# Input weights of a hybrid mixer: the low part made by a negated cast on ScalarE and an adding DMA instead of a subtract on VectorE

## The chip, the cores and the metric

The kernel runs on one core of one Trainium2 chip. The metric is the device time in microseconds of one execution of the whole program. Engines are named as in the profile: PE is the matrix engine (TensorE), DVE is VectorE, ACT is ScalarE, POOL is GpSimd, SP issues most of the DMAs.

## The reference, cut to what matters

One inference step of a decoder block runs on 512 prompt tokens and 8 sample tokens (520 columns, handled as two halves of 260): a half-step SwiGLU feed-forward network (FFN), a mixer, a second FFN, and a final norm. The change touches the first product of the mixer:

```python
def _hybrid_mixer(h, pool_prefix, conv_prefix, ssm_h0, start_pos, w_in, ...):
    proj = h @ w_in
    u_pool, z, xbc, dt_raw = jnp.split(proj, [POOL_DIM, POOL_DIM + SSD_DIM, ...], axis=-1)
    pool_out, new_pool = _pool_mix(u_pool, ...)
    xbc_act, new_conv = _causal_conv(xbc, ...)
    ...
    return cat @ w_out, ...
```

`w_in` has 1024 rows. Its columns, apart from the 16 of `dt`, are 24 blocks of 128: 4 for B and C (bc0 to bc3), 8 for x (x0 to x7), 4 for the pooling mixer (p0 to p3) and 8 for the gate z (z0 to z7). Everything is float32 and has to be accurate to nearly that.

## The kernel before, in words

PE multiplies numbers of the shorter type float32r at one fast pass. To keep accuracy, each operand is split in a high part (the value cast to float32r) and a low part (the rest), and a product is three products: high by high, high by low, low by high (`mm3`, lines 121 to 126). The activations of the mixer are split in `prep` (lines 140 to 146): ScalarE writes `xh` (line 143), VectorE writes `xl` (line 144).

One block of `w_in` is one unit: a weight tile of 128 partitions by 1024 columns, 512 KB. `inproj` (line 709) loads it with `load_unit` (line 116) and issues 48 matmuls of 260 columns: two halves, eight blocks of 128 rows, three products each. In them `whi` stands in lines 122 and 125 and `wlo` in line 126. `load_unit` takes a raw tile, starts the load from SP's queue (line 118), and hands the tile to `split`. `split` (line 101) casts it on ScalarE to `whi` (line 106), and makes the low part in one of two ways. Without `late`, VectorE subtracts the cast from the raw tile (line 113). With `late`, ScalarE writes the negative of the cast of the raw tile into `wlo` (line 109), and a DMA from POOL's queue reads the weights in DRAM a second time and adds them to that tile (line 110); the sum is the same rest. Both FFNs use the second way already for a part of their tiles, in pieces of 128 x 512 or 128 x 384. The mixer's input weights and output weights use the first.

The tags `whi` and `wlo` have three buffers each, so a unit takes the buffer of the third unit before it, once PE is through with that. Raw tiles come in pairs: two units share one allocation of two halves, and there are two such pairs, so a raw pair is loaded again once both its halves have been read.

The order of the mixer's stages is written by hand in three plans. The first, `CONV_PLAN`, starts

```python
    "b0 b1 d0 b2 b3 x0 x1 v0 d1 x2 x3 d2 X0 p0 y0 c0 A0 p1 x4 m0 x5 B0 c1 p2 m1 A1 x6 c2 p3 A2 B1 x7 "
```

where b, x and p are the units above with what follows them (convolution with a ring of columns that POOL prepares, lines 796 to 812; pooling sums on POOL, lines 828 to 846), A and B are the two halves of the state space scan for one chunk and head group (`ssd_a`, `ssd_b`), and c and m are the centring and mixing of the pooling branch. `GATE_PLAN` interleaves the z units with the rest of the scan, the sample tokens (s), the gates (G, H) and the output product (o, g); `LAST_PLAN` ends the mixer and starts the second FFN. A scheduler then places the instructions on each engine's queue, so the order on an engine differs from the written one; every engine works its own queue strictly in order. Before the first unit stand the `dt` products (lines 734 to 739), which need the last chunk of `xh` and `xl`, and the banks of PSUM that the first FFN's last evacuations (line 478) leave.

Banks of PSUM are emptied by VectorE: a unit by lines 719 to 721 (or 1051 for z), the scan's transposes by line 1008 and others, an output product by line 1061.

Of the kernel before, what the change touches and what calls it, by code (L numbers as in the profile page):

```python
# [17 lines left out]
D = 1024  # L18
# [43 lines left out]
def tile_trunk_step(ctx: ExitStack, tc: tile.TileContext, ins: dict, outs: dict):  # L62
# [7 lines left out]
    wp = ctx.enter_context(tc.tile_pool(name="wp", bufs=3, side="right"))  # L70
# [24 lines left out]
    def raw_tile(name):  # L95
        if not half:
            t = raw_pair(name)
            half.extend([t[:, 1], t[:, 0]])
        return half.pop()

    def split(src, n, name, hp, nb, tags, late=None):
        hi, lo = (hp.tile([P, 1024], F32R, tag=t, bufs=nb, name=f"{t}_{name}")[:, :n] for t in tags)
        h, l = hi, lo
        if len(src.shape) == 3:
            h, l = (t.rearrange("p (j c) -> p j c", j=src.shape[1]) for t in (hi, lo))
        nc.scalar.copy(h, src)  # L106
        q = 0 if late is None else n - late.shape[1]
        if late is not None:
            nc.scalar.activation(out=lo[:, q:], in_=src[:, q:], func=AF.Copy, scale=-1.0)
            nc.gpsimd.dma_start(out=lo[:, q:], in_=late, accum_op=ALU.add)  # L110
        if late is None or q:
            s = slice(0, q) if late is not None else slice(None)
            nc.vector.tensor_tensor(out=l[:, s], in0=src[:, s], in1=h[:, s].bitcast(F32), op=ALU.subtract)
        return hi, lo

    def load_unit(src, n, name):
        raw = raw_tile(name)[:, :n]
        nc.sync.dma_start(out=raw, in_=src)
        return split(raw, n, name, wp, 3, ("whi", "wlo"))

    def mm3(ps, whi, wlo, xhi, xlo, start, stop, pin=False, **kw):
        first = nc.tensor.matmul(ps, whi, xhi, start=start, stop=False, **kw)  # L122
# [81 lines left out]
    class Ffn:  # L204
# [257 lines left out]
        def down(self, c, lo, hi, after):  # L462
            n = hi - lo
            banks, units = {}, {}

            def part(d, ks):
                if d not in units:
                    units[d] = load_unit(ins[f"w{self.i}d"][d, :, lo * P : hi * P], n * P, f"{self.i}d{d}_{c}")
                    banks[d] = ps[0].tile([P, 2, 512], F32, tag="BE", bufs=2, name=f"dn{self.i}_{d}_{c}")
                wh, wl = units[d]  # L470
                for b in range(2):
                    for k in ks:
                        g = self.g[lo + k]
                        mm3(banks[d][:, b, :HB], ws(wh, k), ws(wl, k), g[:, 0, b], g[:, 1, b], k == 0, k == n - 1)

            def done(d):
                for b, hs in enumerate(HALVES):
                    nc.vector.tensor_tensor(out=h[:, d, hs], in0=banks[d][:, b, :HB], in1=h[:, d, hs], op=ALU.add)
                    after(d, b, hs)

            part(0, range(n - 1))
            part(1, range(n - 1))
            part(0, range(n - 1, n))
            done(0)
            part(1, range(n - 1, n))
            done(1)
            for d in range(2, KD):
                part(d, range(n))
                done(d)
# [139 lines left out]
    todo, late = [], []  # L629
# [48 lines left out]
def mixer(tc, ins, outs, e):  # L678
    nc = tc.nc
    cst, act, wp, tmp, dr, pool = (e[x] for x in ("cst", "act", "wp", "tmp", "dr", "pool"))  # L680
    ones = e["ones"]
    bank, load_unit, mm3, ws, v, rstd, rstds, vec, h, nx2, raw_tile, open_f2, fin, fill = (
        e[x] for x in ("bank", "load_unit", "mm3", "ws", "v", "rstd", "rstds", "vec", "h", "nx2", "raw_tile",
                       "open_f2", "fin", "fill"))
# [22 lines left out]
    ncp = mp.tile([P, 12, 3], F32, tag="ncp", name="ncp")  # L707

    def inproj(src, name):
        wh, wl = load_unit(src, D, f"in{name}")  # L710
        bs = [bank(f"in{name}{b}") for b in range(2)]
        for b, hs in enumerate(HALVES):
            for k in range(KD):
                mm3(bs[b][:, :HB], ws(wh, k), ws(wl, k), xh[:, k, hs], xl[:, k, hs], k == 0, k == KD - 1)
        return bs
# [111 lines left out]
    def pooling(g):  # L827
        w = WINDOWS[g]
        bs = inproj(ins["w_in"][12 + g], f"p{g}")
        U = cv[0].tile([P, LP], F32, tag="cu", bufs=6, name=f"PU{g}")  # L830
        us = U[:, SAMPLE_P:LP].rearrange("p (b j) -> p b j", j=16)
# [214 lines left out]
    def zproj(j):  # L1046
        if not zbox:
            zbox.append(cv[0].tile([P, NX, NT], F32, tag="zs", name="zs"))
        bs = inproj(ins["w_in"][16 + j], f"z{j}")
        for b, hs in enumerate(HALVES):  # L1050
            nc.vector.tensor_tensor(out=zbox[0][:, j, hs], in0=bs[b][:, :HB], in1=r[:, hs], op=ALU.mult)
# [55 lines left out]
    def outs_a():  # L1107
# [4 lines left out]

    stages = {
        "b": lambda j: conv(8 + j, inproj(ins["w_in"][j], f"bc{j}"), BC[:, j]),
        "x": lambda j: conv(j, inproj(ins["w_in"][4 + j], f"x{j}"), X[:, j]),
        "d": lambda j: box.update(dta=token_dt()) if j == 0 else (token_acs(box["dta"]), sample_decay()) if j == 1 else head_acs(),
# [118 lines left out]
```

## Time and profile before

| what | value |
|---|---|
| median of three runs | 984.54 us (983.57 to 985.28) |
| the profiled execution | 984.47 us |
| its span, first to last instruction | 982.6 us |
| granted clock of PE, mean | 0.997 |
| busy share PE, DVE, ACT, POOL | 97%, 89%, 69%, 22% |
| DMA | 145.46 MB moved, mean 148 GB/s |

A row of a timeline gives the start in us from the span's start, the length in us, the engine, the line, the operation, the tile written and the tiles read, the shape, the count, and in brackets how long the engine had been idle and what ended that. A row of stretches gives the stretch, its length, the busy time of PE, of the weight loads of PE, of DVE, ACT and POOL with counts, the granted clock, the busy share of the DMA engines and the GB/s. A row of groups gives the line, engine and operation, the count, and after the bar the busy time, the mean length of one in ns and the idle time before them. A DMA row gives the issues, the KB of each and the median us from issue to landing.

### The profile page before, as it was taken

Reading aid. Unit: us, or ns where it says so; the run is one execution under the profiler, and the core shown is the slowest. Engines: PE = TensorE matmul, PEld = TensorE weight load, DVE = VectorE, ACT = ScalarE, POOL = GpSimd, SP = SyncE. Lnnn points to the kernel's source line nnn. Section 1 sums busy time; section 2 is a strip of 40 time slices with the busy share of each in tenths; the row PEclk is TensorE's granted clock in tenths of the full one; section 3 lists DMA queues with packets and bytes.
Section 4 is the critical chain, followed back from the end, with each engine's and each line's share of the span. In section 5 each row is a group of like instructions: output and inputs, shape, how many; then the busy total and the mean of one; then the engine's idle time right before and its main releaser. Section 6 shows DMA issues by size and latency. Waiting matters only on the chain.

```text
span 982.6 us, 20242 instructions
## 1 busy us (share of the span) xinstructions
PE 951.5 (97%) x7636; PEld 927.4 (94%) x7636; DVE 877.8 (89%) x1624; ACT 678.2 (69%) x1263; POOL 217.9 (22%) x319
## 2 busy tenths in 40 slices
PE   7999999999999999999999999999999999999995
PEld 6899999999999999999899998989999999999995
DVE  7899899989989698788979987999999999999976
ACT  7677677677777475685754335678788888888864
POOL 0112211121121000157411000113333233233300
PEclk9999999999999999999999999999999999999998
DMA  5565766576566243262335232456687768767732
GB/s 182 161 172 114 191 161 143 133 186 175 124 149 165 65 148 119 87 210 86 115 120 165 96 115 90 106 152 164 164 213 185 183 156 223 190 155 189 190 91 88
DMA packets 63571, 145.46 MB, mean 148 GB/s; under 512 B 9257, under 2 KB 22505, under 8 KB 63473
## 3 DMA queue, kind: packets, MB, share of 16 engines
q1 hardware_dynamic: 41168, 103.78, 33.2%
q0 software_dynamic: 22304, 40.38, 22.5%
q8 instruction: 60, 0.98, 0.4%
q14 instruction: 39, 0.31, 0.1%
HBM read 136.80 MB, written 7.34 MB: 147 GB/s over the span
## 4 chain that ended last, share of the span: by engine, by line
PE 85%; DVE 8%; ACT 3%; issue 2%; DMA 1%; POOL 1%; SPq 0%; DVEq 0%; ACTq 0%
PE A L126 7%; PE A L122 7%; PE A L125 7%; PE BE L122 6%; PE BE L125 6%; PE BE L126 6%; PE P L311 3%; PE wo L122 2%; PE wo L125 2%; PE wo L126 2%; PE inz L122 2%; PE A2d L125 2%; PE A2d L126 2%; PE A1d L125 2%; PE A1d L126 2%
## 5 line engine op out<-in xcount | busy, mean ns | idle before, releaser
L380 ACT COPY ac<-A 128x260 f32<-128x260 f32 x123 | 45.1, 369 | 16.8 <-PE A L126 16.5
L311 PE MATMUL P<-xg_f,raw 128*128 128x260 f32 x192 | 45.9, 398 | 5.5 <-DMA raw<-in_w1gu 5.5
L346 DVE TENSOR_TENSOR s<-raw 128x1024 f32<-128x1024 f32 x41 | 49.8, 1216 | 1.4 <-DMA raw<-in_w2gu 1.4
L311 PEld LDWEIGHTS P<-xg_f,raw 128*128 128x128 f32 x192 | 37.5, 199 | 11.5 <-ACT xg_f L188 5.4
L943 POOL DMA_DIRECT2D out_nss<-hs x32 | 20.6, 643 | 79.2 <-DVE hs L961 74.0
L106 ACT CAST whi_wo<-raw_wo 128x1024 fp32r<-128x1024 f32 x12 | 12.5, 1046 | 36.5 <-issue 9.2
L125 PE MATMUL wo<-catg,whi_wo 128*128 128x260 f32 x128 | 36.4, 285 | 1.3 <-DVE catg L1092 1.3
L122 PE MATMUL wo<-catg,whi_wo 128*128 128x260 f32 x128 | 37.3, 292 | 0.3 <-DVE h L1061 0.3
L122 PE MATMUL inz<-xh_mx,whi_inz 128*128 128x260 f32 x128 | 36.8, 288 | 0.0
L122 PE MATMUL inx<-xh_mx,whi_inx 128*128 128x260 f32 x128 | 36.4, 285 | 0.0
L126 PE MATMUL wo<-catg,wlo_wo 128*128 128x260 f32 x128 | 36.3, 284 | 0.0
L126 PE MATMUL inz<-xh_mx,wlo_inz 128*128 128x260 f32 x128 | 36.2, 283 | 0.0
L126 PE MATMUL inx<-xh_mx,wlo_inx 128*128 128x260 f32 x128 | 36.2, 283 | 0.0
L125 PE MATMUL inz<-xl_mx,whi_inz 128*128 128x260 f32 x128 | 36.2, 283 | 0.0
L125 PE MATMUL inx<-xl_mx,whi_inx 128*128 128x260 f32 x128 | 36.1, 282 | 0.0
L392 DVE TENSOR_TENSOR tg<-BE,ac 128x520 f32<-128x520 f32 x41 | 28.3, 691 | 5.2 <-PE BE L126 5.2
L807 DVE SCALAR_TENSOR_TENSOR A<-U,h,A 128x544 f32<-128x544 f32 x36 | 28.0, 778 | 4.3 <-ACT A L805 3.3
L401 DVE TENSOR_TENSOR tg<-tg,r_f 128x520 f32<-128x520 f32 x41 | 28.4, 694 | 1.3 <-ACT tg L399 1.0
L398 DVE TENSOR_TENSOR tg<-tg,r_f 128x520 f32<-128x520 f32 x41 | 28.4, 692 | 0.1
L347 DVE TENSOR_TENSOR s<-s,raw 128x512 f32<-128x512 f32 x41 | 28.0, 682 | 0.0
L348 DVE TENSOR_TENSOR s<-s,raw 128x512 f32<-128x512 f32 x41 | 27.9, 681 | 0.0
L399 ACT ACTIVATE tg<-tg 128x520 f32<-128x520 f32 x41 | 26.1, 637 | 1.0 <-DVE tg L398 0.9
(1787 smaller groups left out, 4747.4 us busy)
## 6 DMA issues: line engine op xcount, KB each, us to landing
raw<-in_w2gu SPq DMA_DIRECT2D x44, 512.0 KB, 4.9
raw<-in_w1gu SPq DMA_DIRECT2D x42, 512.0 KB, 4.7
raw_1d<-in_w1d SPq DMA_DIRECT2D x24, 384.0 KB, 4.0
raw_2d<-in_w2d SPq DMA_DIRECT2D x24, 384.0 KB, 4.0
raw_wo<-in_w_out SPq DMA_DIRECT2D x12, 512.0 KB, 4.8
ab<-scr_acs SPq DMA_DIRECT2D x8, 512.0 KB, 4.4
h<-in_state_ssm SPq DMA_DIRECT2D x16, 256.0 KB, 3.8
raw_inz<-in_w_in SPq DMA_DIRECT2D x8, 512.0 KB, 4.1
```

The lines of the kernel that those rows point to most:

```text
L122: first = nc.tensor.matmul(ps, whi, xhi, start=start, stop=False, **kw)
L125: nc.tensor.matmul(ps, whi, xlo, start=False, stop=False, **kw)
L126: nc.tensor.matmul(ps, wlo, xhi, start=False, stop=stop, **kw)
L311: nc.tensor.matmul(self.banks[f, u][b][:, :HB], ws(self.raw[f][:, u], j + 4 * q), xg[:, slot[q]], start=j == q == 0, stop=j == 3 and q == ...
L346: nc.vector.tensor_tensor(out=s1, in0=diag, in1=up0, op=ALU.add)
L347: nc.vector.tensor_tensor(out=s2[:, 0], in0=s1[:, 1], in1=raw[:, 0, :nb], op=ALU.add)
L348: nc.vector.tensor_tensor(out=s2[:, 1], in0=s2[:, 0], in1=raw[:, 0, nb : 2 * nb], op=ALU.add)
L380: nc.scalar.copy(keep, out[:, :HB])
L392: nc.vector.tensor_tensor(out=tg, in0=self.BE[k][:, :, :HB], in1=a, op=ALU.add)
L398: nc.vector.tensor_tensor(out=tg, in0=tg, in1=r, op=ALU.mult)
L401: nc.vector.tensor_tensor(out=tg, in0=tg, in1=r, op=ALU.mult)
L807: nc.vector.scalar_tensor_tensor(out=A[:, :n], in0=U[:, j : j + n], scalar=w(j), in1=A[:, :n], op0=ALU.mult, op1=ALU.add)
```

## The change

`load_unit` takes a `late` argument and hands it to `split`, and `inproj` gives the weights in DRAM for it, for every unit but bc0. So 23 of the 24 input units get their low part from a ScalarE write of the negated cast (line 109) and an adding DMA of 512 KB from POOL's queue (line 110), and 23 subtracts of line 113 go from VectorE. The output weights keep the subtract. Line numbers stay the same.

```diff
-    def load_unit(src, n, name):
+    def load_unit(src, n, name, late=None):
         raw = raw_tile(name)[:, :n]
         nc.sync.dma_start(out=raw, in_=src)
-        return split(raw, n, name, wp, 3, ("whi", "wlo"))
+        return split(raw, n, name, wp, 3, ("whi", "wlo"), late)
...
     def inproj(src, name):
-        wh, wl = load_unit(src, D, f"in{name}")
+        wh, wl = load_unit(src, D, f"in{name}", None if name == "bc0" else src)
```

The scheduler's new order keeps PE's almost as it was. On ScalarE each negation stands right behind the cast of its unit, except that those of bc1 and bc2 stand one cast earlier, between the last norm chunks. On POOL the 23 issues are spread between the ring copies, the pooling sums and the scan's products. On VectorE the instructions around the 23 subtracts move up.

## The prediction

> **What bounds the kernel now.** I read the page's busy shares first, then its chain of work, then the busy time by stretches, then who waits for whom on PE.
>
> ```profile
> span 982.6 us, 20242 instructions
> PE 951.5 (97%) x7636; PEld 927.4 (94%) x7636; DVE 877.8 (89%) x1624; ACT 678.2 (69%) x1263; POOL 217.9 (22%) x319
> ...
> PE 85%; DVE 8%; ACT 3%; issue 2%; DMA 1%; POOL 1%; SPq 0%; DVEq 0%; ACTq 0%
> ```
>
> PE is busy 97% of the span and is 85% of the chain that ended last. The change gives PE no less work (its matmuls are the same and stand in nearly the same order), so it can only act through PE's waits. How many are there in the mixer (about 360 to 600 us)? The busy time by stretches, columns PE, PEld, DVE, ACT, POOL:
>
> ```profile
> 335.00:420.00 85.00, 82.53 (x679) 80.77 (x678) 68.00 (x143) 51.41 (x92) 7.68 (x35) 1.00 0.31 105
> 420.00:475.00 55.00, 53.79 (x454) 50.70 (x453) 48.67 (x101) 39.09 (x82) 36.66 (x58) 1.00 0.46 151
> 475.00:530.00 55.00, 54.58 (x458) 51.55 (x459) 49.50 (x140) 32.73 (x60) 12.02 (x12) 1.00 0.39 126
> 530.00:632.00 102.00, 98.86 (x748) 93.50 (x747) 89.58 (x215) 46.78 (x62) 6.76 (x7) 1.00 0.33 104
> ```
>
> PE idles 2.5, 1.2, 0.4 and 3.1 us: 7.2 us in 297. That is the ceiling of any gain. VectorE is 80 to 90% busy, ScalarE 46 to 71%: the work moves from the fuller engine to the emptier one, but neither sets the end; PE does. PE's waits one by one, in the order of time:
>
> ```profile
> 360.74 0.29 PE L737 MATMUL dt<-xh_mx,w 128*48 128x260 f32 x1 [1.35 <-DVE dt_v L757]
> ...
> 472.53 1.09 PE L1027 MATMUL yd<-ab,xdt 128*64 128x128 f32 x16 [0.35 <-DVE U L719]
> 474.20 0.30 PE L976 MATMUL pb<-ident,BC 128*128 128x128 f32 x1 [0.58 <-DVE U L721]
> 475.38 0.55 PE L984 MATMUL px<-ident,X 128*128 128x128 f32 x3 [0.66 <-DVE xdt L1008]
> 579.03 1.15 PE L168 MATMUL psr_y<-X,ones 128*128 128x260 f32 x4 [1.56 <-ACT X L1083]
> 595.07 0.39 PE L125 MATMUL wo<-catg,whi_wo 128*128 128x260 f32 x1 [0.62 <-DVE catg L1092]
> 598.55 0.39 PE L125 MATMUL wo<-catg,whi_wo 128*128 128x260 f32 x1 [0.63 <-DVE catg L1092]
> 599.58 0.39 PE L122 MATMUL wo<-catg,whi_wo 128*128 128x260 f32 x1 [0.28 <-DVE h L1061]
> ```
>
> No wait is for an input weight: those tiles are ready early. Seven of the eight are for VectorE, which the change relieves.
>
> **What the change removes and adds.** The subtracts it removes and the casts that stay, each as the busy time of one line in one stretch (stretch, its length, busy time and count, clock, DMA share, GB/s), and a small precedent:
>
> ```profile
> 360.00:515.00 155.00, 30.04 (x23) 1.00 0.37 123
> ...
> 360.00:515.00 155.00, 23.26 (x23) 1.00 0.37 123
> L109 ACT ACTIVATE wlo_3a<-raw 128x512 fp32r<-128x512 f32 x1 | 0.6, 625 | 0.0
> ```
>
> The first row is line 113 alone: 23 subtracts, 30.0 us of VectorE. The second is line 106: 23 casts, 1.01 us each. The new ScalarE write has half-size precedents at 625 ns (third row); between that and twice that, 1.25 us, I take the cast's 1.04 us: 23 x 1.04 = 24 us more on ScalarE. On POOL come 23 issues, bounded and priced by these rows:
>
> ```profile
> L110 POOL DMA_DIRECT2D wlo_1b<-in_w1gu x1: 846/846/846, 31.4 to 31.4; - x1
> ...
> DMA to landing us min/median/max: 3.4/4.9/9.2
> raw_inz<-in_w_in SPq DMA_DIRECT2D x8, 512.0 KB, 4.1
> raw_1d<-in_w1d SPq DMA_DIRECT2D x8, 256.0 KB, 3.2
> wlo_1a<-in_w1gu POOLq DMA_DIRECT2D x1, 256.0 KB, 3.9
> ```
>
> An issue holds POOL 0.85 us (20 us in all). No adding DMA of 512 KB is in the trace. An adding one of 256 KB took 3.9 us, and doubling a plain load cost 4.1 - 3.2 = 0.9 us, so I take 4.8, say 5 us, with 3.4 and 9.2 (the ends of the 126 existing ones) as bounds.
>
> The Trainium skill, "DMA: Bandwidth & Descriptors", section "Anatomy of one DMA — SWDGE (gpsimd) path", fits about 2.0 us plus bytes/436e3 for a DMA issued from GpSimd; by that estimate 512 KB would land in 3.2 us, below the fastest 256 KB one here (3.4), so the trace's rows decide. With 3.2 us the sum stays as it is and only the slower rival loses weight.
>
> **Does the longer path reach PE?** The low tiles have three buffers, so a unit's buffer is freed when the third unit before it is done. The tightest is x1, which takes over from bc2:
>
> ```profile
> 383.88 0.28 PE L126 MATMUL inbc<-xh_mx,wlo_inbc 128*128 128x260 f32 x1
> ...
> 395.75 0.28 PE L126 MATMUL inx<-xh_mx,wlo_inx 128*128 128x260 f32 x1
> ```
>
> bc2 ends at 383.88 + 0.28 = 384.16, and x1's first low product comes at 395.75: 11.6 us. The new path is cast 1.04, negation 1.04, DMA 5: 7.1 us. Cover is left of 4.5 us; with a landing of 9.2 it is 11.3, still inside. Units further on have transposes and scan products between them and more room. In POOL's new order each of these DMAs stands behind the ring copies of the unit before (0.2 us each) and ahead of the evacuation copies, and later behind the pooling sums. The longest such queue is before p2:
>
> ```profile
> 435.56 0.64 POOL L843 TENSOR_TENSOR PW<-PW,rcnt 128x3 f32<-128x3 f32 x1
> 440.76 0.29 PE L126 MATMUL inp<-xh_mx,wlo_inp 128*128 128x260 f32 x1
> ```
>
> p2's DMA now follows that line 843, which ended at 436.2. Two more issues (x4, x5) stand before it, but the products it waits for come from a less loaded VectorE (two subtracts fewer, 2.6 us), so I put its issue at about 435 and its landing at 440: in time by under 1 us. Bounds: 0, and 3 us of PE wait if the issue slips to 438.5. I take 0; behind the issue on POOL stand the sums of p1 and the copies of x4, which PE does not need soon.
>
> **Step 1, the seam from the first FFN: a loss.** Two negations (bc1, bc2) now stand on ScalarE ahead of the last two norm chunks:
>
> ```profile
> 357.38 0.51 ACT L143 ACTIVATE xh_mx<-h 128x260 fp32r<-128x260 f32 x1
> ...
> 359.31 1.04 ACT L106 CAST whi_inbc<-raw_inbc 128x1024 fp32r<-128x1024 f32 x1 [0.39 <-PE dn L125]
> ...
> 359.84 0.75 DVE L478 TENSOR_TENSOR h<-dn,h 128x260 f32<-128x260 f32 x2
> 360.30 0.51 ACT L143 ACTIVATE xh_mx<-h 128x260 fp32r<-128x260 f32 x1
> ...
> 362.00 0.48 DVE L144 SCALAR_TENSOR_TENSOR xl_mx<-h,xh_mx 128x260 fp32r<-128x260 f32 x1
> ```
>
> The chunk cast at 357.38 moves to 358.4, the one at 360.30 by both negations less the idle 0.39 before the second cast, to about 362. Its low part, no longer behind a subtract, goes from 362.00 to 362.45 and ends at 362.9. PE's dt products start when line 478 frees the banks; VectorE's new order puts that ahead of one low part, so about 0.4 us earlier (360.35). Fourteen products at 0.12 us (54.58 us over 458 in the stretches above) bring PE to 362.05, where it waits for the low part until 362.95: 0.9 lost, 0.4 won, **+0.5 us**. Bounds: -0.4 (no wait) and +1.7 (all of the delay).
>
> **Step 2, the waits at 472 to 475: a gain.** VectorE is behind by then:
>
> ```profile
> 461.24 1.99 DVE L113 TENSOR_TENSOR wlo_inz<-raw_inz,whi_inz 128x1024 fp32r<-128x1024 f32 x1
> ...
> 473.56 0.41 DVE L720 TENSOR_TENSOR U<-inx,r_mx 128x252 f32<-128x252 f32 x1
> ...
> 474.64 0.68 DVE L1008 TENSOR_TENSOR xdt<-px,tok 128x512 f32<-128x512 f32 x1
> ```
>
> VectorE empties x7's bank only at 473.6 to 474, and the next transposes wait. Without the subtracts of p3, x7, z0 and z1 (4 x 1.3 us, 30.04 over 23) it comes there earlier, and in its new order the evacuation is ahead of four of the scan's subtractions. The 0.35 + 0.58 + 0.66 go: **-1.6 us**. Bounds: 0 and -1.6.
>
> **Step 3, the last gate: part of the waits.** At 579.03 PE waits for squares that ScalarE makes after a weight cast, itself tied to PE's release of a buffer, and after the gate products:
>
> ```profile
> 577.40 1.04 ACT L106 CAST whi_wo<-raw_wo 128x1024 fp32r<-128x1024 f32 x1 [4.73 <-DVE X L1075]
> 578.35 2.60 ACT L1083 ACTIVATE X<-zs 128x520 f32<-128x520 f32 x4
> 589.68 1.21 DVE L113 TENSOR_TENSOR wlo_wo<-raw_wo,whi_wo 128x1024 fp32r<-128x1024 f32 x1
> 596.62 1.21 DVE L113 TENSOR_TENSOR wlo_wo<-raw_wo,whi_wo 128x1024 fp32r<-128x1024 f32 x1
> ```
>
> That cast and its order stay, so I leave the 1.56 us where it is. After it, the new VectorE order takes the subtract at 596.62 from ahead of the last gated low part (the 0.63 goes), and one evacuation from ahead of the first (part of the 0.62; I take 0.37): **-1.0 us**. Bounds: 0 and -3.1 (all four waits).
>
> Sum: 0.5 - 1.6 - 1.0 = -2.1 us. The profiled execution took 984.47 us (1.87 around its span), close to the median of 984.54. 984.47 - 2.1 = **982.4 us**.
>
> **Rivals.**
> - More: the gates end early enough that the 1.56 us goes too: 982.4 - 1.6 = 980.8. For it: the subtracts of z6 and z7 (2.7 us) leave VectorE's last crowded stretch. Against it: the cast at 577.40.
> - No gain: 24 us more in order on ScalarE make its products late where VectorE's were, and the waits only change their name: 984.47 + 0.5 = 985.0, up to 986. For it: ScalarE is 71% busy from 420 to 475 (row above). Against it: of PE's waits above, one names ScalarE, and that one late.
> - Slower: the adding DMAs land late, beside 1 MB raw loads that each second negation sets free. It decides from a path of 11.6 us, thus a landing plus POOL wait above 9.5 us after the negation. With 10.2 us each of the seven back-to-back units bc3 to p1 waits up to 0.7 us: 7 x 0.7 = 5, time 982.4 + 5 = 987.4. For it: the 9.2 in the row. Against it: the median of 4.9 and a DMA share of 0.3 to 0.46 here.
> - VectorE holds POOL: if the scan's tensor_scalar runs kept POOL from issuing for as long as they last (8 of them, 2.2 us), p2 would leave at 437 and PE wait about 1.3 us: 983.7.
>
> ```profile
> 427.45 2.19 DVE L1003 TENSOR_SCALAR ab<-ab,tok 128x128 f32<-128x128 f32 x8
> ```
>
> The Trainium skill, "SBUF — State Buffer", section "Who interferes with whom", says that tensor_scalar can take a mode that locks GpSimd out of the shared port, descriptor generation included. No issue stands beside such a run in this trace, so it shows neither.
>
> **How the numbers follow.** Forecast 0.47 (own range 981.0 to 983.8), more 0.13, no gain 0.15, VectorE holding POOL 0.08, slower 0.17. 0.2% of 984.54 is 1.97 us, about what a measurement of this kernel tells from no change: faster is below 982.57, slower above 986.51. Faster: 0.30 of the forecast's 0.47 and all of "more": 0.43. Same: 0.17, 0.08, and 0.11 of "no gain": 0.36. Slower: 0.04 and 0.17: 0.21. The range 980.5 to 987.0 leaves out about 0.05 below and 0.10 above.
>
> **What would show it.** Right: no PE wait on an input weight's DMA; the rows at 472 to 475 without their waits; a dt product waiting about 0.9 us; 23 POOL issues landing in 4.5 to 7 us. Wrong: PE's weight loads waiting for the low tiles, above all at p2 and x1; ScalarE named in new waits between 420 and 480; landings above 9 us.

## The result, and the profile after

| | median us (lowest to highest, runs) | profiled execution |
|---|---|---|
| before | 984.71 (983.57 to 985.68, 6) | 984.47 |
| after | 990.14 (989.37 to 993.55, 6) | 989.69 |

The changed kernel is 0.6% slower: the ratio is 1.0061, 95% interval 1.0045 to 1.0077. The prediction was 982.4 in a range of 980.5 to 987.0. From the page of after: span and instructions, busy time by engine, and the queue of the DMAs that POOL issues (packets, MB, share of the 16 DMA engines).

```profile
span 987.6 us, 20290 instructions
...
PE 953.9 (97%) x7636; PEld 928.8 (94%) x7636; DVE 854.6 (87%) x1601; ACT 699.9 (71%) x1286; POOL 227.1 (23%) x342
...
q0 software_dynamic: 25616, 52.44, 29.2%
```

The same queue before:

```profile
q0 software_dynamic: 22304, 40.38, 22.5%
```

The work moved as meant: VectorE lost 23.2 us (877.8 - 854.6), ScalarE gained 21.7 (699.9 - 678.2). The queue moved 12.06 MB more and took 288.4 - 221.1 = 67.3 us more of the 16 engines (29.2% of 987.6 less 22.5% of 982.6): 2.9 us for each of the 23 DMAs. What PE waited for between 400 and 605 us, after (line, releaser, total, times, longest):

```profile
PE pm L122 <- ACT catp L853: 2.9, 1, 2.9
PE psr_y L168 <- ACT X L1083: 1.6, 1, 1.6
PE pm L125 <- DVE catp L854: 1.0, 1, 1.0
PE px L984 <- DVE xdt L1008: 1.0, 1, 1.0
PE inz L122 <- DVE E L1037: 0.7, 1, 0.7
PE inp L126 <- DMA wlo_inp<-in_w_in: 0.4, 1, 0.4
PE wo L125 <- DVE catg L1092: 0.4, 1, 0.4
PE yd L1027 <- DVE U L719: 0.2, 1, 0.2
```

The first and third rows are new and are one place: `pm`, the first mixing product of the pooling branch (m0 in the plan, between x4 and x5). Before, it waited for nothing. Its rows in the timeline of after, put together from PE, ScalarE, VectorE, POOL and SP (start, length, engine, line):

```profile
414.05 0.26 ACT L887 ACTIVATE sdec<-sdec 128x64 f32<-128x64 f32 x1 [3.04 <-DVE sdec L886]
...
420.26 1.68 SPq L986 DMA_DIRECT2D ab<-scr_acs  x3
...
426.71 0.21 POOL L990 TENSOR_TENSOR we<-ab,tok 128x8 f32<-128x8 f32 x1 [2.19 <-DMA ab<-scr_acs]
...
427.91 1.27 ACT L996 ACTIVATE E<-ab 64x512 f32<-64x512 f32 x2 [3.34 <-DMA ab<-scr_acs]
...
428.54 0.19 POOL L844 TENSOR_TENSOR PW<-PW,PU 128x1 f32<-128x1 f32 x1
...
433.87 0.60 ACT L853 CAST catp<-PW 128x512 fp32r<-128x512 f32 x1
434.19 1.27 POOL L839 TENSOR_TENSOR PW<-PW 128x652 f32<-128x652 f32 x1
...
434.50 1.51 DVE L854 TENSOR_TENSOR catp<-PW,catp 128x512 fp32r<-128x512 f32 x1 [2.61 <-ACT catp L853]
434.52 0.50 PE L122 MATMUL pm<-catp,wph 128*128 128x260 f32 x2 [2.85 <-ACT catp L853]
```

The same place before:

```profile
418.44 1.27 SPq L986 DMA_DIRECT2D ab<-scr_acs  x3
...
425.54 1.26 ACT L996 ACTIVATE E<-ab 64x512 f32<-64x512 f32 x2
...
428.95 0.71 ACT L853 CAST catp<-PW 128x8 fp32r<-128x8 f32 x2
...
431.97 0.28 PE L122 MATMUL pm<-catp,wph 128*128 128x260 f32 x1
```

`ab` is the scan's decay, read back from DRAM in three loads of 512 KB (`ssd_a`). After, these are issued 1.8 us later (the store of `scr_acs` that they wait for took 3.1 us to land, 1.8 before) and take longer. From issue to landing (smallest, median, largest), after, where the trace tells the landing of the second and the third load alone:

```profile
DMA to landing us min/median/max: 7.3/7.6/7.9
```

and before, of all three:

```profile
DMA to landing us min/median/max: 3.4/5.5/7.0
```

The second and third took 5.5 and 7.0 us before, 7.3 and 7.9 after. ScalarE stood idle for 3.34 us in front of E, which reads `ab`, and the cast that PE needs (line 853) stood behind E in its queue. The lateness begins ahead of `ab`: the small store of `scr_dt`, beside p0's adding DMA, took 2.7 us to land (1.3 before), the loads of `sdt` wait for it, VectorE's line 886 reads `sdt`, and ScalarE stood idle 3.04 us for that (the row at 414.05; 0.36 before). The copy that the store of `scr_acs` takes stands behind it in ScalarE's queue. The second wait, put on VectorE, has another part: line 854 took 1.51 us beside POOL's line 839, and the same product took 0.68 in p1_x4_only (last section).

The wait has a second price. Stretches of after (columns as in the prediction; the granted clock is the third number from the end):

```profile
432.00:434.00 2.00, 0.00 (x0) 0.00 (x0) 0.00 (x0) 2.00 (x8) 2.00 (x4) 1.00 1.08 276
434.00:436.00 2.00, 0.50 (x2) 0.30 (x2) 1.50 (x2) 2.00 (x4) 2.00 (x5) 1.00 0.78 213
436.00:438.00 2.00, 1.93 (x9) 1.93 (x10) 2.00 (x7) 2.00 (x5) 1.03 (x4) 0.51 0.04 12
438.00:440.00 2.00, 2.00 (x13) 2.00 (x13) 1.38 (x6) 2.00 (x6) 1.44 (x6) 0.64 0.68 47
```

After the pause PE runs for 3.4 us at half its clock (0.51 and 0.64 as means of these stretches): x5's 48 products take 6.68 us from first to last start, 5.62 before. Against before, the start of each unit's first product goes -1.49 us at bc0 (of which -1.09 was there at the last products of the first FFN; z6_z7_only, which changes nothing so early, shows -0.92 there), -0.42 at x4, **+4.41 at x5**, +5.47 at p2, +5.68 at z0, and +4.8 after the last gate. Nearly the whole loss is made between x4's end and x5's end.

### The profile page after: what moved, and what is told of

It is laid out like the page before. It is cut to its first block, busy times and chain, and to the rows that moved or that the text cites. A ratio compares the mean times of both kernels' runs of the same rounds, so it can differ in the third digit from the quotient of the medians.

```text
span 987.6 us, 20290 instructions
## 1 busy us (share of the span) xinstructions
PE 953.9 (97%) x7636; PEld 928.8 (94%) x7636; DVE 854.6 (87%) x1601; ACT 699.9 (71%) x1286; POOL 227.1 (23%) x342
## 3 DMA queue, kind: packets, MB, share of 16 engines
q0 software_dynamic: 25616, 52.44, 29.2%
## 4 chain that ended last, share of the span: by engine, by line
PE 81%; DVE 10%; ACT 3%; DMA 3%; issue 2%; SPq 0%; DVEq 0%; ACTq 0%
PE A L126 7%; PE A L122 7%; PE A L125 7%; PE BE L122 6%; PE BE L125 6%; PE BE L126 6%; PE wo L122 2%; PE wo L125 2%; PE wo L126 2%; PE inz L122 2%; PE A2d L125 2%; PE A2d L126 2%; PE A1d L125 2%; PE A1d L126 2%; PE A2d L122 2%
```

## The experiments

Each run says whether the scheduler orders the instructions anew or the order is held. "Order held" means that each engine's instructions are chained in a recorded order by edges that order the issue and wait for nothing:

```diff
+    for a, b in zip(seq, seq[1:]):
+        tc.add_manual_dep(b, a.name, mybir.DependencyInfo(NoSync, DATA), reason="order")
```

Theory T at the start: the adding DMAs fill the DMA engines, so `ab` is late, and ScalarE, which works in order, passes that to PE. R1: the added 22 us on ScalarE do it. R2: ScalarE's new order does it by itself. All times, with the ratio to the kernel before on the same chip:

| run | median us | ratio, 95% interval |
|---|---|---|
| dma16 | 983.74 | 0.9991, 0.9982 to 1.0000 |
| catp_first | 990.23 | 1.0055, 1.0039 to 1.0071 |
| old_neworder | 988.28 | 1.0041, 1.0025 to 1.0057 |
| only_z | 986.39 | 1.0015, 1.0006 to 1.0024 |
| order3 | 989.32 | 1.0044, 1.0030 to 1.0059 |
| near2 | 986.13 | 1.0016, 1.0005 to 1.0026 |
| plain_write | 984.62 | 1.0000, 0.9988 to 1.0012 |
| not_p1_x4_x5_p2 | 986.18 | 1.0015, 1.0002 to 1.0027 |
| order4 | 987.83 | 1.0037, 1.0025 to 1.0048 |
| p1_x4_only | 991.59 | 1.0067, 1.0054 to 1.0079 |
| z6_z7_only | 983.68 | 0.9990, 0.9981 to 0.9998 |
| ends | 983.36 | 0.9988, 0.9979 to 0.9997 |

**dma16: the transfers taken away, everything else kept (order held).**

```diff
-            nc.gpsimd.dma_start(out=lo[:, q:], in_=late, accum_op=ALU.add)
+            k = 16 if late.shape[1] == 1024 else n - q
+            nc.gpsimd.dma_start(out=lo[:, q : q + k], in_=late[:, :k], accum_op=ALU.add)
```

> The changed kernel with the order of every engine's instructions held as it is, and each of the 23 adding DMAs cut from 1024 columns to 16 (left out: the weights are not added to 98% of each low tile). Theory T (the adding DMAs fill the DMA engines, the loads of ab and sdt land later, and ScalarE, in order, holds the first mixing product): ab lands in 4.4 us instead of 6.5, the row of E at 427.9 no longer waits 3.3 us, the wait before pm shrinks from 3.9 to under 1 us, and the time falls by 4 to 6 us to 984 to 986. Rival R1 (the 24 us of added ScalarE writes do it): the wait stays at 3.5 to 4 us, time 989 to 990. Rival R2 (ScalarE's new order does it alone): the same 989 to 990.

Measured: 983.74 us, 6.4 less than the changed kernel. `pm` waits for nothing. The rows of ScalarE and SP (this kernel has one line more, so line 887 is 888 and 996 is 997):

```profile
411.55 0.26 ACT L888 ACTIVATE sdec<-sdec 128x64 f32<-128x64 f32 x1
...
416.52 1.32 SPq L987 DMA_DIRECT2D ab<-scr_acs  x3
...
423.01 1.27 ACT L997 ACTIVATE E<-ab 64x512 f32<-64x512 f32 x2
...
428.98 0.60 ACT L854 CAST catp<-PW 128x512 fp32r<-128x512 f32 x1
```

`ab` is issued 3.7 us earlier than in the changed kernel, E starts 4.9 us earlier without a wait, and the cast follows. The expected landing in 4.4 us did not come: the second and third load took 5.0 and 7.5 us. Most of the gain is in the earlier issue, since `sdt` is there when ScalarE comes to it (the row at 411.55 has no wait). ScalarE has all its new writes and the very same order here, so R1 falls, and R2 in its plain form too. With this order and without the transfers, the change would have brought about 1 us; the interval just reaches no change.

**catp_first: only ScalarE's order mended (order held, the two casts of line 853 ahead of E).**

```diff
 order of ScalarE:
-bt, E, cd, we, ab, catp 8, ab x3, E, cd, ab, we, ab x4, catp 512, ...
+bt, catp 512, catp 8, E, cd, we, ab x4, E, cd, ab, we, ab x4, ...
```

> The changed kernel with the order of every engine held, but on ScalarE the two casts of line 853 for the first pooling block moved from behind the work on ab to ahead of the first E (line 996). All work and all DMAs stay. T: E still waits about 3.3 us for ab and ab still lands in 6.5 us, but the wait before pm goes (at most 0.5 us left), and with it the lowered clock in x5: time 984 to 985.5. R1: the cast comes no earlier than ScalarE's load lets it, wait over 2 us, 988 to 990. R2: as T, 984 to 985.5, since the order is undone.

T's number failed: 990.23 us, nothing won. The cast now stands first and waits by itself:

```profile
428.67 0.72 ACT L853 CAST catp<-PW 128x512 fp32r<-128x512 f32 x2 [5.99 <-POOL PW L844]
```

Its input ends with line 844 on POOL, and there that line stands behind line 990, which reads `ab` (the rows of after above: 426.71, then 428.54). PE still waited 3.7 us, now put down to VectorE's line 854, behind work on `ab` in VectorE's queue. So the pooling chain stands behind `ab` on three engines, and mending one moves the name of the wait, not the time.

**old_neworder: the kernel before, with ScalarE's new order around that place (order held).**

```diff
 order of ScalarE:
-we, ab x4, bt, ab, E, cd, E, cd, ab, we, catp 8, catp 512, ab x4
+bt, E, cd, we, ab, catp 8, ab x3, E, cd, ab, we, ab x4, catp 512, ab
```

> The kernel before, with the order of every engine held as it was, but ScalarE's 20 instructions around the first mixing product in the order that they have in the changed kernel (E and cd of chunk 1 first, the cast of line 853 behind four more activations of ab). T: ab lands in time here, so the cast comes 0 to 1.5 us later and the step loses 0 to 1.5 us: 984.5 to 986. R1: 984.5. R2: the wait of 2.9 + 1.0 us appears before pm and the time is 988.5 to 990.

Measured: 988.28, against T's 984.5 to 986 and near R2. `ab` is in time (E waits 0.76), yet the cast starts at 430.92, and VectorE's line 854 at 433.24, where before it started at 431.09; PE waits 2.79 us. So order alone can cost 3 us when `ab` is issued at 418.5. But this kernel mixes ScalarE's new order with VectorE's old one, in which line 854 stands behind a product that needs ScalarE's last `exp`, so it says how tight the place is rather than what the change did. Together with dma16: the changed kernel's own orders are harmless if E can start at 423, as it does there, and cost if it starts at 427.9. T alone is too simple; it is lateness times order.

**only_z: the change for the z units alone (scheduler's own order).**

```diff
-        wh, wl = load_unit(src, D, f"in{name}", None if name == "bc0" else src)
+        wh, wl = load_unit(src, D, f"in{name}", src if name[0] == "z" else None)
```

> The changed way for the eight z units alone; bc, x and p units keep VectorE's subtract. Nothing is changed up to the first mixing product. T, R1, R2 all: no wait before pm, as before. The last gate keeps its gain of 0.9 us and z units beside a fuller DMA lose 0 to 0.5: 983.5 to 984.8. If instead the adding DMAs cost PE something wherever they stand, z units lose over 1 us: above 985.5.

Measured: 986.39, the last case of the expectation by its number, but not by its reason: no product waits for a low tile. The profiled execution (988.01 us) is the slowest of the eleven. In it `pm` does not wait, the gate's gain is there (+4.02 to +3.13 us against before), but from 472 to 478 us PE's waits grow to 1.22, 0.99 and 0.36 us, and then the clock falls (stretches of only_z):

```profile
476.00:478.00 2.00, 1.16 (x4) 0.76 (x5) 2.00 (x5) 2.00 (x7) 1.07 (x3) 0.51 0.36 133
...
480.00:482.00 2.00, 2.00 (x11) 2.00 (x10) 1.93 (x6) 1.55 (x6) 0.20 (x1) 0.50 0.80 168
```

z0 took 8.00 us, 5.75 before: 2.25 us lost to the clock. It is a second, separate loss (last section). Why the waits grow was not tried. The trace shows VectorE slower beside POOL on the way to them: the four products of line 1041 took 4.24 us (2.61 before), as POOL's issue of a z unit's DMA had moved its line 839 beside them.

**order3 and order4: the order mended on three engines, then one DMA more (orders held).** T2: `pm` is late since `ab` is late and the pooling chain stands behind it on POOL, ScalarE and VectorE.

```diff
 order3: ahead of the first work on ab:
+POOL    L843, L844 (PW, block 0)
+ScalarE L853 x2 (catp, block 0)
+VectorE L854 x2 (catp, block 0)
 order4: as order3, and ahead of the first L990:
+POOL    L110 (wlo of x5)
```

> The changed kernel, all work and all DMAs kept, orders held; for the first pooling block alone the sums' last products on POOL (lines 843 and 844), both casts on ScalarE (line 853) and both subtracts on VectorE (line 854) are moved ahead of the work on ab on their engines. Theory T2 (late ab loads times the place of the pooling chain behind ab on three engines): ab still lands in 7 to 8 us and E still waits, but the wait before pm falls from 3.9 to 0.5 us or less, PE's clock stays at 1.0, time 985 to 986.5. Rival R4 (late ab reaches PE anyway, a few products later): a wait of 2 to 4 us before pst or yd instead, 988 to 990.

> As order3, and on POOL the adding DMA of x5 also stands ahead of the first product on ab (line 990), behind which it waited there. All work and all DMAs are kept. Theory T3 (what is late is what stands behind ab in order: the pooling chain, then x5's adding DMA): the 3.3 us wait of x5's low products goes, no other wait over 1 us appears before z0, time 984 to 986. Rival R4 (some next thing behind ab is late, or x5's DMA beside the ab loads makes these later still): a wait of 2 us or more before pst, yd or p2, 987.5 to 990.

PE's longest wait around x5 in order3, and then the one in order4 with POOL's issue of that tile's DMA:

```profile
435.08 0.39 PE L126 MATMUL inx<-xh_mx,wlo_inx 128*128 128x260 f32 x1 [3.25 <-DMA wlo_inx<-in_w_in]
```

```profile
425.08 0.90 POOL L110 DMA_DIRECT2D wlo_inx<-in_w_in  x1
...
434.50 0.39 PE L126 MATMUL inx<-xh_mx,wlo_inx 128*128 128x260 f32 x1 [1.62 <-DMA wlo_inx<-in_w_in]
```

T2 was right on the mechanism (in both, `pm` waits for nothing) and wrong on the time: 989.32. As soon as `pm` is on time, x5's own low tile is the next thing late, by 3.25 us; its DMA had been issued at 426.1, behind line 990. This is R4 in kind and in time, though at x5's low products and not at `pst` or `yd`. With that DMA ahead of line 990, 1.62 us remain: it was issued at 425.1 and released PE at 434.5, 9.4 us later. The late low tile of the prediction's slower rival is real, but it hid behind a larger delay. T3's 984 to 986 failed too (987.83, inside R4's range): order takes 2.3 us of the loss of 5.4 away. What PE still waits for there, up to p2, are low tiles that land late: 0.21 us at x1, 1.62 at x5, 0.56 at p2.

**near2 and p1_x4_only: which of the 23?** In near2 (order held) the DMAs of p1 and x4 alone are cut; p1_x4_only (scheduler's order) makes the change for these two alone.

```diff
 near2:
+            k = 16 if name in ("inp1", "inx4") else n - q
 p1_x4_only:
+        wh, wl = load_unit(src, D, f"in{name}", src if name in ("p1", "x4") else None)
```

> The changed kernel, orders held, the adding DMA cut to 16 columns for p1 and x4 alone (left out: most of the added weights of these two); the other 21 stay whole. T2 with a local cause (these two are in flight beside the store of scr_acs and the loads of ab): ab lands in 5 to 6.5 us instead of 7.3 to 7.9, the wait before pm is 0 to 1.5 us, time 985 to 987. If the delay is gathered from all DMAs since x0 (sdt, raw tiles): wait still over 2.5 us, 988.5 to 990.

> The changed way for p1 and x4 alone, the other 22 units keep VectorE's subtract; output whole. With it the scheduler already gives ScalarE and POOL the changed kernel's order around the first mixing product. T3: these two adding DMAs with that order are enough: wait before pm 3 to 4 us, time 988 to 990 (no gain at the gate). If the loss needs the load of all 23: wait under 1.5 us, 984.5 to 986.

In near2 E starts at 423.2, PE waits 0.15 us before `pm`, and the time is 986.13 with the other 21 DMAs whole; 1.5 us of what its trace loses is the clock at z0 again (7.27 us). p1_x4_only is as slow as the full change, 991.59, above its range:

```profile
426.84 0.21 POOL L990 TENSOR_TENSOR we<-ab,tok 128x8 f32<-128x8 f32 x1 [2.34 <-DMA ab<-scr_acs]
...
428.51 1.27 ACT L996 ACTIVATE E<-ab 64x512 f32<-64x512 f32 x2 [4.96 <-DMA ab<-scr_acs]
...
435.12 0.38 PE L122 MATMUL pm<-catp,wph 128*128 128x260 f32 x1 [1.78 <-ACT catp L853]
437.00 0.39 PE L125 MATMUL pm<-catp,wph 128*128 128x260 f32 x1 [1.50 <-DVE catp L854]
```

With two of the units changed, the scheduler already chooses nearly the new order, `ab` is late, and the same wait stands at the same place, clock included (0.53 and 0.62 behind it). These two are in flight beside the store of `scr_acs`, which took 5.7 us to land here (1.8 before), and the loads of `ab`. p1_x4_only changes transfers and order together, so alone it would not tell them apart; near2 holds the order. Taking the two away removes the loss at `pm`, and having only them makes it: that settles the place.

**plain_write: is it the adding or the bytes (order held)?**

```diff
-            nc.gpsimd.dma_start(out=lo[:, q:], in_=late, accum_op=ALU.add)
+            nc.gpsimd.dma_start(out=lo[:, q:], in_=late, accum_op=ALU.add if late.shape[1] < 1024 else ALU.bypass)
```

> The changed kernel, orders held, the 23 DMAs of 512 KB write instead of adding (left out: the negated cast is overwritten). If it is the adding that makes them heavy: they land in 5 to 6 us like the raw loads, ab in about 5, wait before pm under 1 us, time 984 to 986. If it is the 12 MB as such: landing 7 to 8.5 us, wait 3 to 4 us, 989 to 990.

Measured: 984.62, no loss. The queue's row and two rows of the DMA issues:

```profile
q0 software_dynamic: 25616, 52.44, 26.1%
...
wlo_inx<-in_w_in POOLq DMA_DIRECT2D x8, 512.0 KB, 5.8
...
wlo_inp<-in_w_in POOLq DMA_DIRECT2D x4, 512.0 KB, 4.1
```

and those of the changed kernel:

```profile
wlo_inx<-in_w_in POOLq DMA_DIRECT2D x8, 512.0 KB, 8.4
...
wlo_inp<-in_w_in POOLq DMA_DIRECT2D x4, 512.0 KB, 6.4
```

The same 52.44 MB, but 256.9 us of the DMA engines instead of 288.4 (26.1% of 984.1): a writing DMA of 512 KB takes (256.9 - 221.1) / 23 = 1.56 us of all 16, an adding one 2.9, and lands 2.3 to 2.6 us later. POOL's issue takes 0.53 us instead of 0.86 (medians of the x units). The expected landing of `ab` in about 5 us did not come (6.2 and 8.3 for the second and third load), but `ab` was issued at 416.73, 3.5 us earlier than in the changed kernel: the gain is in the store and the loads ahead of it. The Trainium skill, "Collectives: The Full Stack", section "The bandwidth ceiling: the fold count and why AG ≠ RS ≠ AR", says that ReduceScatter is slower than AllGather because its add needs two source reads, and measures a ratio of 1.93. That is another kind of transfer; the 1.9 here agrees with it in size, and no run here shows the reason.

**not_p1_x4_x5_p2, z6_z7_only and ends: versions of the change that leave the crowded place alone (scheduler's order).**

```diff
 not_p1_x4_x5_p2:
+        ... None if name in ("bc0", "p1", "x4", "x5", "p2") else src)
 z6_z7_only:
+        ... src if name in ("z6", "z7") else None)
 ends:
+        ... src if name in ("bc1", "bc2", "z4", "z5", "z6", "z7") else None)
```

> The changed kernel, but p1, x4, x5 and p2 keep VectorE's subtract; the scheduler orders it anew (near the first mixing product as in the kernel before). Output is whole. T2: no wait before pm; the last gate keeps its 0.9 us; what only_z lost around 472 to 482 (1 to 3 us) may come again: 984.5 to 987. R4 or a cause elsewhere: over 988.

> The changed way for z6 and z7 alone; output whole. If the gain of 0.9 us at the last gate comes from these two subtracts leaving VectorE: 983.9 to 984.2, and PE's waits before wo shrink as in the changed kernel. If it comes from all the z units' work or from the order: 984.5 to 985.2.

> The changed way for bc1, bc2 and z4 to z7 alone (no adding DMA near the scan's loads); output whole. T3: no wait before pm, waits at 472 to 475 as in the kernel before, dt's wait 0.9 instead of 1.35, the gate's gain 0.9: 983.2 to 984.2, the best whole version so far. If adding DMAs cost PE wherever they are: 985 or more.

The first, 986.18, is inside its range. The expectation of no wait before `pm` failed: it waits 0.9 us, and PE's shift goes from -1.57 us at x4 to -0.42 at x5. z0 takes 7.23 us at a lowered clock, 1.48 more than before. Those two are its losses. The other two are the only whole versions whose intervals lie below the kernel before: 983.68 and 983.36, 0.1% faster. ends has no wait of 0.15 us or more before `pm`, waits 0.7 and 0.5 us at 473 to 475 (`px`, `pb`), and its dt product waits 0.9 us instead of 1.35, as expected.

Two subtracts, z6's and z7's, bring the whole gain at the last gate: 0.89 us with those two alone (-1.56 to -2.45 against before), 0.87 with all 23.

## Why the prediction was wrong

**The step that failed is "Does the longer path reach PE?"** It asked only whether the new low tiles come in time for PE, and answered 0. For the low tiles that was nearly right in the changed kernel: PE lost 1.1 us from bc3 to x4 (shift -1.49 to -0.42), 0.66 of it in p1, whose first low product waited 0.41 us for its tile. What it never asked is what 23 adding DMAs do to the transfers already there: the stores of `scr_dt` and `scr_acs` landed in 2.7 and 3.1 us instead of 1.3 and 1.8, and what waits for them came late. `ab` is three loads of 512 KB, and behind them stand POOL's line 844, ScalarE's 853 and VectorE's 854 in their queues. The price of that place was 4.88 us for the wait (2.85 + 1.04) and the slowed mixing products, and 1.06 us for x5 at a lowered clock. dma16, near2 and p1_x4_only show that the transfers made it, catp_first and order3 that the orders pass it on.

- **"So I take 4.8, say 5 us"** for the landing: measured 5.2 to 9.4, medians 6.4 to 8.5. I doubled a plain load and gave the adding no price. The 3.9 us that I started from was the first adding DMA of the program; the second halves of four later tiles (`wlo_5b`, `6b`, `9b`, `7b`, also 256 KB) took 5.3 to 6.3 us in the same trace. The 3.4 us that I gave as the fastest of 256 KB is one of 192 KB; the fastest of 256 KB took 3.5. The share of the DMA engines, 0.31 to 0.46 over stretches of 55 to 102 us, was an average over crowded and empty places: in single stretches of 2 us the kernel before had 0.98 (414 to 416 us), 1.01 (420 to 422) and 1.07 (422 to 424), just where the DMAs of p1 and x4 and the loads of `ab` fall. There was no room in those stretches.
- **"I put its issue at about 435 and its landing at 440"** (p2): issued at 437.2 and landed 7.3 us later. PE never waited for it in the changed kernel, since `pm` had made PE 5 us late. The neighbour, x5, is the one that would have been late: order4 shows 9.4 us from its issue and 1.62 us of wait.
- **Step 1, +0.5:** measured -0.40 (and the same in dma16). The dt product's wait went from 1.35 to 0.95, and the predicted wait for the last low part did not come; the lower bound (-0.4) was the right end.
- **Step 2, -1.6:** measured +0.2. Even without the adding transfers only 0.56 us was won there (dma16). "VectorE is behind" was a wrong reading: in the kernel before, VectorE stood idle 0.34 us ahead of 466.40, for POOL, and 0.70 us ahead of 470.31, for ScalarE's E, so no delay from the subtract at 461.24 was left by 472. Between then and PE's waits one product of line 1003 took 1.62 us beside POOL's line 839 (0.28 alone), and in the changed kernel another took 1.06 (rows in the last section). No subtract stands in between.
- **Step 3, -1.0:** measured -0.87, and the 1.56 us before `psr_y` stayed, as argued. Right.
- **ScalarE and VectorE:** 24 us more on ScalarE, measured 21.7; 30 less on VectorE, measured 23.2, though all 23 subtracts went. The negation took 1.05 us (predicted 1.04). These sizes did not matter.
- **Rivals.** "Slower" (987.4) had the right sign, and its adding DMAs do land late, but its path was wrong: the units bc3 to p1 lost about 1 us, not 5, and the loss came through other transfers. That its 987.4 lies nearest the result is luck. "No gain" named ScalarE's order, and the wait at `pm` does carry ScalarE's name, but dma16 with the same ScalarE gains. "VectorE holds POOL" did not show: POOL's issue at 427.19 took 0.89 us beside VectorE's tensor_scalar run at 426.95, and 0.86 at 414.81 without one. The reverse shows: POOL's products hold VectorE's (last section).

The result lies 3.1 us above the range. Its upper end counted one late path at a time, with no clock and no second place; the clock alone cost 1.06 us at x5.

## What to carry to other kernels

A DMA that replaces engine work is paid for by the transfers beside it: before pricing it, list what is in flight in the same microseconds, and what stands behind those loads in the in-order queue of every engine, not only who reads the new tile. Here an adding DMA cost nearly twice a writing one. When a scheduler reorders for a load that it believes to be early, look for the critical instruction that has slipped behind that load; and a wait that goes often uncovers the next one a little behind it, so a mend is tried as a whole.

## What the runs showed of the hardware

**The clock falls by PE's idle time in fixed stretches of 3.41 us.** Before x5's products PE paused 1.62 us in order4 and 2.79 us in old_neworder, and the clock stayed at 1.00. After 3.25 us (order3) it fell, and so it did after 1.78 and 1.50 us close together (p1_x4_only). Around z0, where no wait is over 1.22 us, it fell in some kernels and not in others, and the sum of the idle time does not tell which: 1.78 us (not_p1_x4_x5_p2), 1.84 (order3), 1.95 (near2) and 2.57 (only_z) with a fall, 1.88 (the changed kernel) without. The clock's own records do. In all 14 traces every change of the clock lies a whole number of 3.41 us from the first one, and each fall lasts 3.41 us (twice that in only_z). Cut by these edges, the eight stretches ahead of a fall between 12 and 960 us have 1.71 to 2.91 us of idle PE, half of the stretch or more; none of the other 3866 has more than 1.56. In only_z the clock stayed low for a second stretch, behind one with 0.80. Two neighbouring stretches of near2:

```profile
472.64:476.05 3.41, 1.70 (x19) 1.10 (x15) 3.41 (x9) 3.41 (x8) 2.41 (x7) 1.00 0.23 73
476.05:479.47 3.42, 3.42 (x16) 3.42 (x17) 3.25 (x9) 3.42 (x10) 1.26 (x3) 0.50 0.97 161
```

of the changed kernel, with the same two waits (0.99 and 0.72 us) on both sides of an edge:

```profile
476.99:480.41 3.42, 2.26 (x22) 1.24 (x20) 3.42 (x12) 3.16 (x6) 1.65 (x4) 1.00 0.05 8
480.41:483.82 3.41, 2.69 (x21) 2.45 (x22) 3.37 (x8) 3.41 (x12) 2.13 (x3) 1.00 0.76 180
```

and of old_neworder, whose pause of 2.79 us an edge cuts in two:

```profile
430.39:433.80 3.41, 1.95 (x17) 1.74 (x15) 1.92 (x4) 3.41 (x11) 3.21 (x4) 1.00 0.51 157
433.80:437.22 3.42, 2.09 (x17) 2.09 (x18) 3.42 (x7) 3.42 (x7) 2.73 (x5) 1.00 0.00 0
```

A fall costs 1.5 to 2.3 us in z0 (7.23 to 8.00 us instead of 5.75). The first edge lies at 8.4 to 11.8 us from the span's start in the 14 traces, so whether two short waits share a stretch is luck of the execution. The Trainium skill, "TensorE: Matmul & The Clock Gate", section "HAM oscillation — how this bites in real kernels", gives as the rule no idle gaps above some 3.4 us. The traces here do not bear it out: p1_x4_only lost the clock with no pause above 1.78 us.

**POOL's products hold VectorE's.** From the changed kernel, ahead of the wait for line 1008:

```profile
478.59 1.06 POOL L1033 TENSOR_TENSOR hst<-hst,cd 128x512 f32<-128x512 f32 x1
478.67 1.06 DVE L1003 TENSOR_SCALAR ab<-ab,tok 128x128 f32<-128x128 f32 x1
```

The other products of line 1003 there took 0.27 us, and this one ended 0.08 us after POOL's. Line 1041 took 0.34 us alone and 1.41 and 2.07 beside POOL's line 839; line 854 took 0.68 us, and 1.51 beside line 839. Work that is given to POOL, a DMA issue too, moves such meetings. What each cost PE was not tried.

**An adding DMA of 512 KB** took 2.9 us of all 16 DMA engines against 1.56 for a writing one, landed in 8.4 us (median, x units) against 5.8, and held POOL 0.86 us at its issue against 0.53.
